# A hybrid attention layer: matmul operands laid out on 256-byte multiples, and one table of distances for eight heads

## The chip, the cores and the metric

One core of a Trainium2 chip runs the whole layer. The metric is device microseconds of one launch. Of the kernel before there are three times and one profiled execution.

## The reference

512 real tokens with 16 learned tokens put ahead (528 positions), width 2048, one layer. The reference, cut to what matters:

```python
h = concatenate([meta, x]); hn = rmsnorm(h, pre_norm_g)
qa, ka, va, ga, qb, kb, vb, gb = split(hn @ w_in)
# mixer A: 8 query heads on 2 key heads, RMSNorm and rotary on q and k
ya = softmax(q @ k.T / sqrt(128)) @ v * silu(ga)
# mixer B: 8 heads, two score maps of width 64 each; slope_h = 2 ** -(h + 1)
s1 = q1 @ k1.T / 8 - slope_h * abs(qpos - kpos)
s2 = q2 @ k2.T / 8 - slope_h * abs(qpos - kpos)
yb = rmsnorm((softmax(s1) - lam * softmax(s2)) @ v, sub_g) * silu(gb)
y = concatenate([ya, yb]) @ w_out
out = (h + rmsnorm(y, post_norm_g))[16:]
```

## The kernel before

All products are made in 32-bit "fp32r" pairs: an operand is split into a high part (a rounded copy, made on ACT) and a low part (what is left, made on DVE), and a product is three matmuls, high·high, low·high and high·low, into one PSUM bank (`three`, L191). So names end in `h` and `l`: `xh`, `xl` are the layer input (16 tiles each, one for each 128 rows of the width, `k` = 0 to 15), `wh`, `wl` a chunk of weights (`wsplit`, L155, from the loaded chunk `st`), `oh`, `ol` the gated heads.

The stages, in order of time:

- **Projection of keys and values** (`dense_T(KEYS)`, L205): weights stand still in TensorE, `xh`/`xl` stream past in two halves of 264 columns (528 positions), into `pd`, in one place into `sc`.
- **Projection of B queries and gates** (`dense_T(REAL)`): the same with the 512 real columns `xh[k][:, NM:]`, which begin 16 columns (64 bytes) into the tile.
- **Projection of A queries** (`queries_A`, L638): `xh`/`xl` stand still, 512 columns of weights stream.
- **Attention** of each head beside these: scores into `sc` (264 columns), turned by `tr` matmuls (128 columns), then `pv` (256 columns). `attention_B` (L440) loads its head's table `dist` of 912 fp16 numbers in each partition (L442) and adds it to the scores on DVE (L460, `p<-sc,dist`).
- **Output projection** (from L804 on): `oh`/`ol` stand still, 512 columns of weights stream into `po`. `dense_out` makes two of the four column blocks plainly; the other two go through a scheme with sums of operands and fewer products (`product`, L899): seven calls, of which `of_y` uses `oh`/`ol`, and `of_t` the sums `uh`, `ul`, `vh`, `vl`.

TensorE's order is fixed by `Lanes`, which weaves the attention of a head into the projection of the next by written estimates of time (`LAG`); it is kept as program order. A list scheduler orders DVE and ACT, with rank for the weight splits. Loads go out in order on SP's queue.

Tiles of a pool are laid end to end in each partition, each rounded up to 32 bytes; pools made with `side="right"` (`xp`, later `op` in its place) are filled back from the top of the memory. `pad` takes a small tile only to shift what follows. So a tile's address follows from the sizes ahead of it: `xh` tiles of 528 numbers are 2112 bytes, 8.25 times 256, and four neighbours begin at four different offsets within 256 bytes.

Of the kernel before, what the change touches and what calls it, by code (L numbers as in the profile page):

```python
# [10 lines left out]
F32 = mybir.dt.float32  # L11
F32R = mybir.dt.float32r
F16 = mybir.dt.float16
AF = mybir.ActivationFunctionType
ALU = mybir.AluOpType
AX = mybir.AxisListType

P = 128
DM = 2048
KT = DM // P  # L20
SEQ = 512
NM = 16
NT = SEQ + NM
# [5 lines left out]
DW = NT + (TT - 1) * P  # L29
# [79 lines left out]
def kernel(ctx: ExitStack, tc: tile.TileContext, xT, xn, xm, w_s, w_t, w_q, w_o,  # L109
                             gpre, gq, gk, lams, gsub, gpost, ident_d, cos_d, sin_d, dist_d, out):  # L110
    nc = tc.nc
# [5 lines left out]
    cst = ctx.enter_context(tc.tile_pool(name="cst", bufs=1))  # L117
# [13 lines left out]
    def ctile(shape, name, dt=F32, src=None, pool=cst):  # L131
        t = pool.tile(shape, dt, name=name, tag=name, bufs=1)
        if src is not None:
            load(t, src)
        return t

    def pad(pool, name):

        pool.tile([P, 8], F32, name=name, tag=name, bufs=1)

    def load(out, in_):

        tc.keep_in_program_order(nc.sync.dma_start(out=out, in_=in_))
# [23 lines left out]
    warm = ctile([P, 1], "warm")  # L167
    nc.scalar.activation(warm, epst, AF.Identity)

    heat = ctile([P, 256], "heat", F32R, pool=ap)  # L170
    nc.vector.memset(heat.bitcast(F32), 0.0)
    hot = pd.tile([P, 512], F32, name="hot", tag="pd")
    for i in range(16):
        mm(hot[:, :256], heat[:, :P], heat, start=True, stop=True)
    gcol = ctile([P, KT], "gcol")
    nc.scalar.dma_start(out=gcol, in_=gpre)
    xh = [xp.tile([P, NT], F32R, name=f"xh{k}", tag=f"xh{k}") for k in range(KT)]
    xl = [xp.tile([P, NT], F32R, name=f"xl{k}", tag=f"xl{k}") for k in range(KT)]
    pad(xp, "xpad")

    def xload(k):
        st = ap.tile([P, NT], F32, name="xs", tag="p", bufs=6)
# [6 lines left out]
    REAL = [(NM, NT)]  # L189
# [15 lines left out]
    def dense_T(segs, pss=None, half=None):  # L205

        pss = pss or [pd.tile([P, 512], F32, name="pd", tag="pd") for _ in segs]
        for k0 in range(0, KT, 8):
            wh, wl = fetch()
            for k in range(k0, k0 + 8):  # L210
                c = slice((k - k0) * P, (k - k0 + 1) * P)
                for (n0, n1), ps in zip(segs, pss):
                    three(ps[:, :n1 - n0], wh[:, c], wl[:, c], k, n0, n1)
                    lanes.poll()
                if half and k == 10:
                    half()
        return pss
# [14 lines left out]
                for (n0, n1), ps in zip(segs, pss):  # L232
                    three(ps[:, :n1 - n0], wh[:, c], wl[:, c], k, n0, n1)

    ones = ctile([P, P], "ones")
    nc.vector.memset(ones, 1.0)
    ones_r = ctile([P, P], "ones_r", F32R)
    nc.vector.memset(ones_r.bitcast(F32), 1.0)
    mhalf = ctile([P, 8], "mhalf")
    nc.vector.memset(mhalf, -0.5)  # L240

# [23 lines left out]
    nc.vector.tensor_tensor(out=rm, in0=ssm[:, 0:1], in1=ssm[:, 1:2], op=ALU.add)  # L265
    rstd(rt, rt, DM)
    rstd(rm, rm, DM, NM)
    pad(cst, "ipad")
    ident = ctile([P, P], "ident", src=ident_d)
    rB = ctile([P, NT], "rB")  # L270
    dg = ap.tile([P, NT], F32, name="dg", tag="tT")
# [14 lines left out]
    sinT = ctile([P, TT, P], "sinT", src=sin_d, pool=ap)  # L286
    gqB = ctile([P, P], "gqB", src=gq, pool=ap)
    gkB = ctile([P, P], "gkB", src=gk, pool=ap)
    pad(cst, "spad")
    sgc = ctile([P, 1], "sgc", src=gsub)  # L290
    nc.vector.tensor_scalar(out=sgc, in0=sgc, scalar1=1.0 - LAMBDA_INIT, scalar2=None,
                            op0=ALU.mult)

    lmt = ctile([P, 4, 64], "lmt", src=lams)
    lpr = ctile([P, 2, 64], "lpr")
    nc.vector.tensor_tensor(out=lpr, in0=lmt[:, 0::2, :], in1=lmt[:, 1::2, :], op=ALU.mult)
    lsm = ctile([P, 2], "lsm")
    nc.vector.tensor_reduce(out=lsm, in_=lpr, op=ALU.add, axis=AX.X)
    nc.scalar.activation(lsm, lsm, AF.Exp)
# [26 lines left out]
        lo(s2[L], kf[U], s2[U])  # L326
        return s1, s2

    def queries_B(pss):
        qf = ap.tile([P, NT], F32, name="qf", tag="tT")  # L330
        qf = qf[:, :SEQ]
        nc.vector.tensor_tensor(out=qf, in0=pss[0], in1=rB[:, NM:], op=ALU.mult)
        q1 = ap.tile([P, SEQ], F32R, name="q1", tag="q1")
        q2 = ap.tile([P, SEQ], F32R, name="q2", tag="q2")
        l1 = ap.tile([P, SEQ], F32R, name="l1", tag="ql", bufs=4)
        l2 = ap.tile([P, SEQ], F32R, name="l2", tag="ql", bufs=4)
        hi(q1[L], qf[L])
        hi(q2[U], qf[U])
        hi(q1[U], qf[L])
        hi(q2[L], qf[U])  # L340
        lo(l1[L], qf[L], q1[L])
        lo(l2[U], qf[U], q2[U])
        lo(l1[U], qf[L], q1[L])
        lo(l2[L], qf[U], q2[U])
        return (q1, l1), (q2, l2)
# [92 lines left out]
        return t.rearrange("p (a b) -> p a b", a=2)  # L438

    def attention_B(h, qs, ks, v, v_task):  # L440
        dist = ap.tile([P, DW], F16, name="dist", tag="dist")
        nc.sync.dma_start(out=dist, in_=dist_d[h])  # L442
        o = ap.tile([P, SEQ], F32, name="oB", tag="f", bufs=4)
        last = None
        for half in range(2):
            pts = []
            for t in (2 * half, 2 * half + 1):
                tq = slice(t * P, (t + 1) * P)
                mx = ap.tile([P, 2], F32, name="mx", tag="mx", bufs=4)
                sm = ap.tile([P, 2], F32, name="sm", tag="sm", bufs=4)  # L450
                p2 = []
                yield from room(2)
                for m, ((q, ql), s) in enumerate(zip(qs, ks)):
                    sc = psc.tile([P, 2, 512], F32, name="sc", tag="sc")
                    for i, (n0, n1) in enumerate(KEYS):
                        mm(sc[:, i, :HALF], q[:, tq], s[:, n0:n1], start=True, stop=False)
                        mm(sc[:, i, :HALF], ql[:, tq], s[:, n0:n1], start=False, stop=True)
                    p = ap.tile([P, NT], F32, name="p", tag="p", bufs=6)
                    w0 = (TT - 1 - t) * P
                    nc.vector.tensor_tensor_reduce(  # L460
                        out=two(p), in0=sc[:, :, :HALF], in1=two(dist[:, w0:w0 + NT]),
                        scale=-0.125, scalar=3.0e38, op0=ALU.add, op1=ALU.min,
                        accum_out=mx[:, m:m + 1])
                    p2.append(p)
                    if m == 0:
                        yield LAG["scB"]
                for m in range(2):
                    nc.scalar.activation(p2[m], p2[m], AF.Exp, scale=-1.0,  # L468
                                         bias=mx[:, m:m + 1], accum_out=sm[:, m:m + 1])
                nc.vector.reciprocal(out=sm, in_=sm)  # L470
                c2 = ap.tile([P, 1], F32, name="c2", tag="c2", bufs=4)
                nc.vector.tensor_tensor(out=c2, in0=sm[:, 1:2], in1=nlam, op=ALU.mult)
                nc.gpsimd.tensor_scalar(out=p2[0], in0=p2[0], scalar1=sm[:, 0:1], scalar2=1.0,  # L473
                                        op0=ALU.mult, op1=ALU.mult)
                nc.vector.scalar_tensor_tensor(out=p2[0], in0=p2[1], scalar=c2, in1=p2[0],
                                               op0=ALU.mult, op1=ALU.add)
                pts.append(p2[0])
                if t % 2 == 0:
                    yield LAG["scB"]
            last = spawn_pv(v_task, p_times_v(pts, v, lambda pv, half=half: nc.scalar.activation(  # L480
                o[:, half * 256:(half + 1) * 256], pv, AF.Copy), None), LAG["pB"])
            if half == 0:
                yield LAG["scB"]
        over[h] = lanes.spawn(finish_B(h, o), LAG["fin"], last)
# [37 lines left out]
    zed = []  # L522
# [52 lines left out]
    def head_norm(raw, n, g, rows=P):  # L575

        ss = ap.tile([P, 4], F32, name="ssh", tag="ssh", bufs=4)
        for i in range(n):
            jk = ap.tile([P, P], F32, name="jk", tag="jk")
            nc.scalar.activation(jk[:rows], raw[:, i, :], AF.Square, accum_out=ss[:rows, i:i + 1])  # L580
        rstd(ss[:rows, :n], ss[:rows, :n], P, rows)
        for i in range(n):
            nc.vector.scalar_tensor_tensor(out=raw[:, i, :], in0=raw[:, i, :],  # L583
                                           scalar=ss[:rows, i:i + 1], in1=g[:rows], op0=ALU.mult,
                                           op1=ALU.mult)
# [15 lines left out]
    def keys_A(pss):  # L601
# [1 line left out]
        for (n0, n1), ps in zip(KEYS, pss):  # L603
            nc.scalar.activation(kf[:, n0:n1], ps[:, :n1 - n0], AF.Copy)
        kn = ap.tile([P, TT, P], F32, name="kn", tag="f", bufs=4)
        km = ap.tile([NM, 1, P], F32, name="km", tag="km")
        kh = ap.tile([P, NT], F32R, name="kh", tag="s1")
        kl = ap.tile([P, NT], F32R, name="kl", tag="s2")

# [128 lines left out]
    sc = psc.tile([P, 2, 512], F32, name="sc", tag="sc")  # L738
    pss = dense_T(KEYS, [sc[:, 0, :], sc[:, 1, :]], spread)
    ks = keys_B(first[0])  # L740
    qs = queries_B(first[1])
    v = values(pss)
    gB = [gate(first[2], "gB0")] + [None] * (NH - 1)
    heads, over = [None] * (2 * NH), [None] * (2 * NH)
# [5 lines left out]
    for h in range(NH):  # L750
        heads[h] = lanes.spawn(attention_B(h, qs, ks, *v), LAG["head"], heads[h - 1])
        if h > 0 and h not in LATE:
            weigh()
            gB[h] = gate(dense_T(REAL), f"gB{h}")
        if h + 1 < NH:
            if h:
                weigh()
            pss = dense_T(KEYS)
            if h:
                finish_head(h - 1)  # L760
            v = values(pss)
            if h:
                weigh()
            ks = keys_B(dense_T(KEYS))
            qs = queries_B(dense_T(REAL))
    kA, vA = [], []
    for i in range(2):
        pss = dense_T(KEYS)
# [1 line left out]
        kA.append(keys_A(pss))  # L770
        vA.append(values(dense_T(KEYS)))
    gA = []
    zed.append(ap.tile([P, DW], F16, name="zed", tag="dist"))
    nc.vector.memset(zed[0], 0.0)
    for grp in range(2):
        qn, q_task = queries_A(grp)
# [14 lines left out]
    op = ctx.enter_context(tc.tile_pool(name="op", bufs=1, side="right", reuse_waits="tile"))  # L791
    oh = [op.tile([P, SEQ], F32R, name=f"oh{j}", tag=f"oh{j}") for j in range(KT)]
    ol = [op.tile([P, SEQ], F32R, name=f"ol{j}", tag=f"ol{j}") for j in range(KT)]
    pad(op, "opad")

    def bring(j):
        st = wp.tile([P, 1024], F32, name="os", tag="st")
# [308 lines left out]
```

## Time and profile before

| | |
|---|---|
| median of 3 runs | 937.16 us (936.48 to 939.98) |
| the profiled execution | 936.8 us, its span 935.0 us |
| TensorE (PE) | 919.7 us busy, 98% of the span, 5498 matmuls |
| weight loads (PEld) | 808.4 us, 86% |
| DVE | 570.8 us, 61% |
| ACT | 489.3 us, 52% |
| POOL | 120.8 us, 13% |
| mean granted TensorE clock | 0.997 |

How to read it: a matmul's busy time is longer than its place in the stream, since matmuls overlap; 512 columns show some 395 ns while the next one starts 230 ns later. What counts is the spacing from start to start, and a row of the chain of waits gives it: its length divided by its count of matmuls. PEld runs beside PE, the weights of the next matmul being loaded while the one before streams.

### The profile page before, as it was taken

Reading aid. Unit: us, or ns where it says so; the run is one execution under the profiler, and the core shown is the slowest. Engines: PE = TensorE matmul, PEld = TensorE weight load, DVE = VectorE, ACT = ScalarE, POOL = GpSimd, SP = SyncE. Lnnn points to the kernel's source line nnn. Section 1 sums busy time; section 2 is a strip of 40 time slices with the busy share of each in tenths; the row PEclk is TensorE's granted clock in tenths of the full one; section 3 lists DMA queues with packets and bytes.
Section 4 is the critical chain, followed back from the end, with each engine's and each line's share of the span. In section 5 each row is a group of like instructions: output and inputs, shape, how many; then the busy total and the mean of one; then the engine's idle time right before and its main releaser. Section 6 shows DMA issues by size and latency. Waiting matters only on the chain.

```text
span 935.0 us, 14280 instructions
## 1 busy us (share of the span) xinstructions
PE 919.7 (98%) x5498; PEld 808.4 (86%) x5498; DVE 570.8 (61%) x1013; ACT 489.3 (52%) x853; POOL 120.8 (13%) x164
## 2 busy tenths in 40 slices
PE   9999999999999999999999999999999999999996
PEld 8989898998989899898999888887888888888884
DVE  6376675747557475765756246447645573654797
ACT  6665564637455474644645244436554662524662
POOL 0001110110101110010111030115211120300110
PEclk9999999999999999999999999999999999999998
DMA  9855534544536365231322223221222163765884
GB/s 336 264 166 146 140 125 117 148 144 134 159 103 180 101 164 150 68 103 68 93 71 87 90 85 96 70 77 57 83 76 69 60 212 94 269 207 160 287 311 181
DMA packets 44260, 129.75 MB, mean 139 GB/s; under 512 B 5120, under 2 KB 9984, under 8 KB 43936
## 3 DMA queue, kind: packets, MB, share of 16 engines
q1 hardware_dynamic: 40784, 117.29, 37.8%
q0 software_dynamic: 3264, 11.54, 6.6%
q8 instruction: 43, 0.70, 0.3%
q14 instruction: 25, 0.20, 0.1%
q10 hardware_dynamic: 144, 0.01, 0.0%
HBM read 120.43 MB, written 25.17 MB: 156 GB/s over the span
## 4 chain that ended last, share of the span: by engine, by line
PE 92%; DVE 3%; issue 1%; ACT 1%; DMA 1%; POOL 0%; DVEq 0%; POOLq 0%; ACTq 0%
PE pd L63 60%; PE po L63 16%; PE sc L63 6%; PE tr L66 5%; PE pv L63 5%; DVE y L995 1%; DMA os<-oscr 1%; DVE wl L159 0%; PE ss L63 0%; DVE l L316 0%; ACT wh L158 0%; DMA gcol<-in_gpre_dram 0%; DVE y L1007 0%; DVE qn L583 0%; POOL ssh L246 0%
## 5 line engine op out<-in xcount | busy, mean ns | idle before, releaser
L63 PE MATMUL pd<-xh,wh 128*128 128x264 f32 (+1 forms) x992 | 332.5, 335 | 0.1
L63 PE MATMUL pd<-xh,wl 128*128 128x264 f32 (+1 forms) x992 | 324.2, 327 | 1.1 <-DVE wl L159 1.0
L63 PE MATMUL pd<-xl,wh 128*128 128x264 f32 (+1 forms) x992 | 324.5, 327 | 0.0
L158 ACT ACTIVATE wh<-st 128x1024 fp32r<-128x1024 f32 (+2 forms) x147 | 152.7, 1040 | 213.5 <-issue 91.5
L159 DVE TENSOR_TENSOR wl<-st,wh 128x1024 fp32r<-128x1024 f32 (+2 forms) x147 | 176.4, 1201 | 120.5 <-ACT wh L158 119.6
L63 PEld LDWEIGHTS pd<-xh,wl 128*128 128x128 f32 x992 | 186.5, 188 | 18.2 <-DVE wl L159 1.5
L63 PEld LDWEIGHTS pd<-xh,wh 128*128 128x128 f32 x992 | 186.9, 188 | 12.8 <-ACT wh L158 0.4
L63 PEld LDWEIGHTS pd<-xl,wh 128*128 128x128 f32 x992 | 187.1, 189 | 11.2 <-DVE xl L185 0.2
L63 PE MATMUL po<-wh,oh 128*128 128x512 f32 x176 | 70.3, 402 | 0.1
L468 ACT ACTIVATE p<-p,mx 128x528 f32<-128x528 f32 x64 | 47.0, 734 | 43.0 <-DVE mx L460 42.7
L63 PE MATMUL po<-wh,ol 128*128 128x512 f32 x176 | 69.0, 395 | 0.2 <-DVE ol L316 0.2
L63 PE MATMUL po<-wl,oh 128*128 128x512 f32 x176 | 69.0, 395 | 0.0
L313 ACT ACTIVATE ph<-tr 128x512 fp32r<-128x512 f32 x64 | 37.7, 590 | 39.1 <-PE tr L66 38.7
L460 DVE CUSTOM_DVE_ANT_0 p<-sc,dist 128x528 f32<-128x528 f32 x64 | 44.8, 700 | 15.3 <-PE sc L63 15.0
L316 DVE TENSOR_TENSOR pl<-tr,ph 128x512 fp32r<-128x512 f32 x64 | 43.4, 687 | 16.6 <-ACT ph L313 16.2
L66 PE MATMUL tr<-ident,p 128*128 128x128 f32 (+1 forms) x320 | 50.6, 272 | 1.7 <-DVE pl L316 1.7
L63 PE MATMUL pd<-wh,xh 128*128 128x512 f32 x128 | 51.9, 406 | 0.0
L63 PE MATMUL pd<-wl,xh 128*128 128x512 f32 x128 | 50.5, 394 | 0.0
L63 PE MATMUL pd<-wh,xl 128*128 128x512 f32 x128 | 50.3, 393 | 0.0
L66 PEld LDWEIGHTS tr<-ident,p 128*128 128x128 f32 (+1 forms) x320 | 37.4, 131 | 13.0 <-DVE pl L316 2.5
L558 POOL TENSOR_SCALAR p<-p,smA 128x528 f32<-128x528 f32 x32 | 26.9, 841 | 144.6 <-DVE smA L557 123.0
L473 POOL TENSOR_SCALAR p<-p,sm 128x528 f32<-128x528 f32 x32 | 23.0, 718 | 168.7 <-DVE sm L470 168.3
(202 smaller groups left out, 1478.2 us busy)
## 6 DMA issues: line engine op xcount, KB each, us to landing
st<-in_w_t_dram SPq DMA_DIRECT2D x82, 512.0 KB, 3.8
st<-in_w_o_dram SPq DMA_DIRECT2D x24, 512.0 KB, 4.0
ws<-in_w_o_dram POOLq DMA_DIRECT2D x16, 512.0 KB, 6.6
st<-in_w_q_dram SPq DMA_DIRECT2D x16, 512.0 KB, 3.5
st<-ws SPq DMA_DIRECT2D x16, 512.0 KB, 4.9
xs<-in_xT_dram SPq DMA_DIRECT2D x16, 264.0 KB, 5.6
xns<-in_xn_dram SPq DMA_DIRECT2D x8, 512.0 KB, 5.2
ws<-in_w_o_dram SPq DMA_DIRECT2D x8, 512.0 KB, 5.3
```

Source lines behind the costliest of these rows:

```text
L63: self._add(self.nc.tensor.matmul(out, lhsT, rhs, start=start, stop=stop), us)
L66: self._add(self.nc.tensor.transpose(out, in_, ident), 0.109)
L158: nc.scalar.activation(wh[:, c], st[:, c], AF.Copy)
L159: nc.vector.tensor_tensor(out=wl[:, c], in0=st[:, c], in1=wh[:, c].bitcast(F32), op=ALU.subtract)
L313: nc.scalar.activation(dst, src, AF.Copy)
L316: nc.vector.tensor_tensor(out=dst, in0=src, in1=h.bitcast(F32), op=ALU.subtract)
L460: nc.vector.tensor_tensor_reduce(out=two(p), in0=sc[:, :, :HALF], in1=two(dist[:, w0:w0 + NT]), scale=-0.125, scalar=3.0e38, op0=ALU.add, ...
L468: nc.scalar.activation(p2[m], p2[m], AF.Exp, scale=-1.0, bias=mx[:, m:m + 1], accum_out=sm[:, m:m + 1])
L473: nc.gpsimd.tensor_scalar(out=p2[0], in0=p2[0], scalar1=sm[:, 0:1], scalar2=1.0, op0=ALU.mult, op1=ALU.mult)
L558: nc.gpsimd.tensor_scalar(out=p, in0=p, scalar1=sm, scalar2=1.0, op0=ALU.mult, op1=ALU.mult)
L995: order(nc.vector.scalar_tensor_tensor(out=v, in0=v, scalar=ry[t], in1=xres[t, g], op0=ALU.mult, op1=ALU.add))
```

## The change

In the built program it moves addresses and leaves TensorE's 5184 rows in the order they had. The offsets below are those of the operands' first byte, modulo 256, worked out from the allocations of both programs; "moving" is the operand that streams, "standing" the one loaded as weights.

| matmuls | moving, standing before | after |
|---|---|---|
| keys, values: 1920 of 264 columns | eight offsets in turn (`xh`/`xl`: 0 and 32, 64 and 96, 128 and 160, 192 and 224), 128 | 192 and 224, 0 |
| B queries, gates: 1152 of 512 | 0, 64, 128 or 192 by `k`, 128 | 0, 0 |
| A queries: 384 of 512 | 128; 0, 64, 128 or 192 by `k` | 0, 0 |
| output with `oh`/`ol`: 528 of 512 | 128, 192 | 0, 0 |
| output with `u`, `v`: 144 of 512 | 128, 128 | 0, 0 |
| last output product, `v`: 48 of 512 | 192, 128 | 0, 0 |
| scores: 448 of 264 | multiples of 32, 128 | multiples of 32, 64 |
| `pv`: 384 of 256 (`ph`/`pl`, `vh`/`vl`) | 0, 128 | 128, 64 |

Room for wider tiles comes from single buffers (`dist`, `jk`, `km`, `zed`), from shared places (`heat` in the place of `pm`, `lmt` in that of `fr`, `ones` and `ones_r` in one) and from the table: head 2's distances (`dist_d[2]`, slope 1/8) are loaded once and serve all eight heads. The B queries are multiplied by `slope(h)` = 2^(h−2) as they leave PSUM, and the scale of L460 is divided by it.

```diff
-    def pad(pool, name):
+    def pad(pool, name, n):
-        pool.tile([P, 8], F32, name=name, tag=name, bufs=1)
+        pool.tile([P, n // 4], F32, name=name, tag=name, bufs=1)
...
-    heat = ctile([P, 256], "heat", F32R, pool=ap)
+    heat = ap.tile([P, 256], F32R, name="heat", tag="pm")
...
-    xh = [xp.tile([P, NT], F32R, name=f"xh{k}", tag=f"xh{k}") for k in range(KT)]
-    xl = [xp.tile([P, NT], F32R, name=f"xl{k}", tag=f"xl{k}") for k in range(KT)]
-    pad(xp, "xpad")
+    xh, xl = [[xp.tile([P, 576], F32R, name=f"x{n}{k}", tag=f"x{n}{k}")[:, :NT]
+               for k in range(KT)] for n in "hl"]
+    pad(xp, "xpad", 32)
...
-    pad(cst, "spad")
+    pad(cst, "spad", 160)
...
+    dist = ap.tile([P, DW], F16, name="dist", tag="dist", bufs=1)
+    pad(ap, "dpad", 32)
+    load(dist, dist_d[2])
+
+    def slope(h):
+        return 2.0 ** (h - 2)
+
-    def queries_B(pss):
+    def queries_B(h, pss):
...
-        nc.vector.tensor_tensor(out=qf, in0=pss[0], in1=rB[:, NM:], op=ALU.mult)
+        nc.vector.scalar_tensor_tensor(out=qf, in0=pss[0], scalar=slope(h), in1=rB[:, NM:],
+                                       op0=ALU.mult, op1=ALU.mult)
...
     def attention_B(h, qs, ks, v, v_task):
-        dist = ap.tile([P, DW], F16, name="dist", tag="dist")
-        nc.sync.dma_start(out=dist, in_=dist_d[h])
...
-                        scale=-0.125, scalar=3.0e38, op0=ALU.add, op1=ALU.min,
+                        scale=-0.125 / slope(h), scalar=3.0e38, op0=ALU.add, op1=ALU.min,
...
-    zed.append(ap.tile([P, DW], F16, name="zed", tag="dist"))
+    zed.append(ap.tile([P, DW], F16, name="zed", tag="dist", bufs=1))
...
-    pad(op, "opad")
+    pad(op, "opad", 224)
```

On SP's queue the constants end with `lmt`, and the weight chunks `st` of the following projections come behind them. Before:

```order
L143 DMA sgc<-in_gsub_dram 128x1
L143 DMA lmt<-in_lams_dram 128x256
L151 DMA st<-in_w_t_dram 128x1024 x3
L442 DMA dist<-in_bias_dram 128x912 x2
L151 DMA st<-in_w_t_dram 128x1024 x5
```

In the changed program:

```order
L143 DMA sgc<-in_gsub_dram 128x1
L143 DMA lmt<-in_lams_dram 128x256
L143 DMA dist<-in_bias_dram 128x912
L151 DMA st<-in_w_t_dram 128x1024 x8
L143 DMA ws_545<-in_w_o_dram 128x1024
```

The one table now stands ahead of three chunks of weights, and the seven other loads of a table are gone from the queue.

On DVE, where the first head's keys are split (`s`) beside the first weights of the next projection (`wl`), the rows before were:

```order
L316 TENSOR_TENSOR s_679<-kf,s_679 64x528
L159 TENSOR_TENSOR wl<-st,wh 128x1024
L316 TENSOR_TENSOR s_680<-kf,s_680 64x528
L316 TENSOR_TENSOR l_689<-qf,q_687 64x512
L159 TENSOR_TENSOR wl<-st,wh 128x1024
```

In the changed program:

```order
L316 TENSOR_TENSOR s_679<-kf,s_679 64x528
L316 TENSOR_TENSOR s_680<-kf,s_680 64x528
L159 TENSOR_TENSOR wl<-st,wh 128x1024
L316 TENSOR_TENSOR l_689<-qf,q_687 64x512
L159 TENSOR_TENSOR wl<-st,wh 128x1024
```

The first `wl` comes one row later, behind both halves of the keys; ACT's rows for the same data (`s` and `wh`) change places in the same way.

More of the change, by code (lines that the diff above doesn't have):

```diff
@@ L233 @@
                     three(ps[:, :n1 - n0], wh[:, c], wl[:, c], k, n0, n1)
-    ones = ctile([P, P], "ones")
+    ones_r = ctile([P, P], "ones_r", F32R)
+    ones = ones_r.bitcast(F32)
     nc.vector.memset(ones, 1.0)
-    ones_r = ctile([P, P], "ones_r", F32R)
-    nc.vector.memset(ones_r.bitcast(F32), 1.0)
     mhalf = ctile([P, 8], "mhalf")
@@ L267 @@
     rstd(rm, rm, DM, NM)
-    pad(cst, "ipad")
+    pad(cst, "ipad", 32)
     ident = ctile([P, P], "ident", src=ident_d)
@@ L292 @@
                             op0=ALU.mult)
-    lmt = ctile([P, 4, 64], "lmt", src=lams)
-    lpr = ctile([P, 2, 64], "lpr")
-    nc.vector.tensor_tensor(out=lpr, in0=lmt[:, 0::2, :], in1=lmt[:, 1::2, :], op=ALU.mult)
+    lmt = ap.tile([P, 4, 64], F32, name="lmt", tag="fr")
+    load(lmt, lams)
+    lpr = lmt[:, 0::2, :]
+    nc.vector.tensor_tensor(out=lpr, in0=lpr, in1=lmt[:, 1::2, :], op=ALU.mult)
     lsm = ctile([P, 2], "lsm")
@@ L578, in head_norm @@
         for i in range(n):
-            jk = ap.tile([P, P], F32, name="jk", tag="jk")
+            jk = ap.tile([P, P], F32, name="jk", tag="jk", bufs=1)
             nc.scalar.activation(jk[:rows], raw[:, i, :], AF.Square, accum_out=ss[:rows, i:i + 1])
@@ L605, in keys_A @@
         kn = ap.tile([P, TT, P], F32, name="kn", tag="f", bufs=4)
-        km = ap.tile([NM, 1, P], F32, name="km", tag="km")
+        km = ap.tile([NM, 1, P], F32, name="km", tag="km", bufs=1)
         kh = ap.tile([P, NT], F32R, name="kh", tag="s1")
@@ L740 @@
     ks = keys_B(first[0])
-    qs = queries_B(first[1])
+    qs = queries_B(0, first[1])
     v = values(pss)
@@ L764 @@
             ks = keys_B(dense_T(KEYS))
-            qs = queries_B(dense_T(REAL))
+            qs = queries_B(h + 1, dense_T(REAL))
     kA, vA = [], []
```

## The prediction

> **What bounds the kernel now.** I read the page's shares first, then the chain of waits, then its pieces inside single stages.
>
> ```profile
> PE 919.7 (98%) x5498; PEld 808.4 (86%) x5498; DVE 570.8 (61%) x1013; ACT 489.3 (52%) x853; POOL 120.8 (13%) x164
> PE 92%; DVE 3%; issue 1%; ACT 1%; DMA 1%; POOL 0%; DVEq 0%; POOLq 0%; ACTq 0%
> ```
>
> PE carries 92% of the chain; no other engine carries more than 3%. So the time is the number of matmuls times their spacing, and a change of addresses can act only through the spacing. Does the spacing depend on addresses? The output projection is the clean place: four stretches of it, one after another, are nothing but 512-column matmuls, and the chain gives length and count (start, length, engine and tile, count).
>
> ```profile
> 799.86 65.33 PE po L63 x280
> 871.96 18.15 PE po L63 x80
> 893.29 10.27 PE po L63 x44
> 904.95 9.76 PE po L63 x43
> ```
>
> The spacings are 233.3, 226.9, 233.4 and 227.0 ns. The first and third stretch read `oh`/`ol` (moving at 128, standing at 192), the second and fourth the sums `u` and `v` (128 and 128). Shape, clock and number of operands are the same, and the spacing goes up and down with the offset. So offsets do cost time. A last stretch has moving 192, standing 128; its first and last row here stand 40 matmuls apart:
>
> ```profile
> 915.47 0.39 PE L63 MATMUL po<-wh,vh 128*128 128x512 f32 x1
> 924.63 0.39 PE L63 MATMUL po<-wh,vl 128*128 128x512 f32 x1
> ```
>
> That is 229.0 ns. I read from it that the difference between the two offsets matters: none gives 226.9, 64 gives 229.0, minus 64 gives 233.3. After the change all 512-column matmuls have difference 0, like the 226.9 stretch, though at 0 and 0 instead of 128 and 128. No matmul at 0 and 0 stands in this trace: that step is an inference.
>
> The remaining 512-column matmuls sit in the projections:
>
> ```profile
> 516.72 56.50 PE pd L63 x243
> 205.54 4.17 PE pd L63 x18
> 436.20 4.20 PE pd L63 x18
> ```
>
> A queries: 232.5 ns. Gates, the first and last of 10 undisturbed 18-matmul pieces in the attention of the B heads: 231.7 and 233.3. I use 232.5 for both. They don't reach 226.9 even where a tile has difference 0, since the offsets change after every 3 or 6 matmuls. Where the `u` stretch begins one sees what a change of offset costs:
>
> ```profile
> 870.87 0.40 PE L63 MATMUL po<-wh,uh 128*128 128x512 f32 x1
> 872.49 0.39 PE L63 MATMUL po<-wh,ul 128*128 128x512 f32 x1
> ```
>
> These are its first and its eighth matmul: seven spacings of 231.4, and only then 226.9. A stream settles.
>
> The Trainium skill, "SBUF — State Buffer", section "SBUF: two separate sides", says that PE has ports of its own and never waits for anyone, and that a port lock between DVE and GpSimd is the only contention on the engine side. By that rule addresses cost nothing and the change gives 937; the four stretches above speak against it, by 6.4 ns a matmul.
>
> **The change part by part.**
>
> *Output projection.* `oh`/`ol` have 528 matmuls. 369 of them stand in the undisturbed stretches (321 in a row, then 48 between the sums): 369 × (233.3 − 226.9) = 2.4 us. The other 159 share PE with the last heads and mostly stay in the first seven after a change: 159 × (233.3 − 231.4) = 0.3 us. The sums in the second and fourth stretch gain nothing. The last product gains 48 × 2.1 = 0.1 us on PE, which I don't count, for the end belongs to DVE:
>
> ```profile
> 914.97 0.60 DVE y L1001
> 922.29 0.60 DVE y L1001
> 930.38 1.32 DVE y L995 x2
> ```
>
> From 914.97 the chain runs on DVE alone. Sum: 2.7 us.
>
> *Gates, B queries, A queries.* 1536 matmuls. In PE's program order, which stays, 570 of them stand later than seventh in a run of their own kind (363 gates and B queries, 207 A queries); the others are in short runs between pieces of attention. 570 × (232.5 − 226.9) + 966 × (232.5 − 231.4) = 3.2 + 1.1 = 4.3 us. Bounds: nothing settles between pieces of attention (all 1536 at 231.4: 1.7 us), or all is settled from the first (226.9: 8.6 us).
>
> *Keys and values.* These 1920 matmuls now all have 192 and 224 against 0. Before, four pairs take turns; `xh2` had that same pair of differences (64 and 96 against 128). One turn from `xh2`, at its four first matmuls and the next `xh6`:
>
> ```profile
> 44.10 0.28 PE L63 MATMUL sc<-xh,wh 128*128 128x264 f32 x1
> 44.83 0.28 PE L63 MATMUL sc<-xh,wh 128*128 128x264 f32 x1
> 45.55 0.29 PE L63 MATMUL sc<-xh,wh 128*128 128x264 f32 x1
> 46.27 0.28 PE L63 MATMUL sc<-xh,wh 128*128 128x264 f32 x1
> 47.00 0.28 PE L63 MATMUL sc<-xh,wh 128*128 128x264 f32 x1
> ```
>
> Six matmuls each: 0.73, 0.72, 0.72, 0.73 us. The pair that remains is one of the dearer: 121.7 against the turn's mean of 2.90 / 24 = 120.8; if it keeps its price, 1920 × 0.9 = 1.7 us are lost. In the output projection difference 64 was not dear once settled, so I take half of this, 0.9 us lost, between 1.5 us gained (all as cheap as 0.72 / 6 = 120.0) and 3.3 us lost (0.73 may be 0.735: 122.5).
>
> *Scores and `pv`.* The score operands still take turns over multiples of 32; `pv` goes from difference 128 to 64. Neither has a long stretch to read. I take 0, ± 0.5 us (800 matmuls, ± 0.6 ns, the spread of the pairs above).
>
> *The table.* Seven loads go. Nobody waited for one: the score operation's idle time is PE's.
>
> ```profile
> L460 DVE CUSTOM_DVE_ANT_0 p<-sc,dist 128x528 f32<-128x528 f32 x64 | 44.8, 700 | 15.3 <-PE sc L63 15.0
> dist<-in_bias_dram SPq DMA_DIRECT2D x8, 228.0 KB, 2.8
> 45.63 1.11 SPq L442 DMA_DIRECT2D dist<-in_bias_dram  x2
> ```
>
> Gain 0. One load moves ahead of three weight chunks on SP: 0.55 us of issue later for them. The multiplication by the slope makes 8 tensor-tensor operations into three-operand ones:
>
> ```profile
> L332 DVE TENSOR_TENSOR qf<-pd,rB 128x512 f32<-128x512 f32 x8 | 5.5, 690 | 30.8 <-PE pd L63 30.8
> L508 DVE SCALAR_TENSOR_TENSOR gB<-oB,sgc,gB 128x512 f32<-128x512 f32 x8 | 5.9, 739 | 0.0
> ```
>
> 8 × 49 ns = 0.4 us on an engine that is 61% busy and sits idle for PE ahead of just this line; the scores of the head come later. 0, at most 0.4. The clearing of `zed` now waits for head 7's last score operation, on the same engine, and A's first score comes after.
>
> *The moved row.* The first `wl` of the next projection now stands behind one more `s`, and PE waits there:
>
> ```profile
> 52.12 0.70 DVE L316 TENSOR_TENSOR s<-kf,s 64x528 fp32r<-64x528 f32 x1
> 52.85 1.22 DVE L159 TENSOR_TENSOR wl<-st,wh 128x1024 fp32r<-128x1024 f32 x1
> 58.93 0.77 DVE L307 TENSOR_TENSOR vf<-sc,rB 128x264 f32<-128x264 f32 x2
> 54.13 0.40 PE L63 MATMUL pd<-xh,wl 128*128 128x264 f32 x1 [0.99 <-DVE wl L159]
> 59.42 0.89 PE L66 MATMUL tr<-ident,vf 128*128 128x128 f32 x4 [1.25 <-DVE vf L307]
> ```
>
> PE starts 0.70 us later at 54.13. But it waits again for `vf` at 59.42, 1.25 us long, and DVE's rows up to `vf` are the same in sum; so the second wait shrinks to 0.55 and the cost is 0. That wait is the cover; were it gone, 0.7 us.
>
> *Sharing bytes.* `oh0` now lies over `xh3` and `xh4` instead of `xh0` and `xh1`, so its first writer must wait for later matmuls.
>
> ```profile
> 741.09 1.39 PE pd L63 x6
> 741.62 0.63 ACT L313 ACTIVATE oh<-os 128x512 fp32r<-128x512 f32 x1
> ```
>
> The last gate ends at 742.48; after `xh4` it has 11 tiles with 3 matmuls, at least 7.7 us at 232.5, so `xh4` was free by 734.8, before that write. Cost 0.
>
> *The sum.* −2.7 − 4.3 + 0.9 = −6.1 us: span 928.9, and the profiled execution's 936.8 becomes 930.7. The median of the runs stands 0.4 us above it, so **931 us**. The ends of the unknown terms together: gains of 2.7 + 8.6 + 1.5 + 0.5 = 13.3, to 924; at the other ends 2.7 + 1.7 − 3.3 − 0.5 − 0.4 = 0.2 is left, 937.
>
> **The rivals.**
>
> *Nothing to measure (935 to 937).* The 6.4 ns belong to something else in the two kinds of stretch, or the 264-column matmuls lose what the others gain: 3.3 + 0.9 us lost against 4.4 gained, if nothing settles. For it: only 369 matmuls have a like-for-like row, and they alone bring 2.4 us. Against it: the stretches alternate twice, between calls of the same function. The skill's rule of the separate ports, above, comes to this rival.
>
> *Much faster (below 924).* Offset 0 removes the rest of the excess as well. From 264 columns at 120.8 to 512 at 226.9 a column costs 0.428 ns, and 512 of these with nothing fixed beside them are 219 ns. The 2208 matmuls on the path have a mean of 232.2 now (1536 at 232.5, 528 at 233.3, 144 at 226.9, with a little rounding): 2208 × 13.2 = 29 us, to 908; half of it 922. For it: each operand then starts on a 256 boundary, which no row has. Against it: 226.9, 229.0 and 233.3 order themselves by difference alone, and nothing settled lies lower. The Trainium skill, "TensorE: Matmul & The Clock Gate", section "Back-to-back issue gap", gives N / 2.4 + 2.5 ns for an isolated warm matmul, 216 ns for 512 columns at any address; by that figure the most to be had would be an estimated 36 us, to 901, and no stretch of this trace agrees with it.
>
> *Slower (above 942).* At 0 and 0 moving and standing stream begin in the same place and hinder each other more than at 128 and 128, all the time since all share it. It decides from a rise of (4.7 − 0.9) / 2208 = 1.7 ns, to a mean of 233.9; at 238 it is 2208 × 5.8 + 0.9 us = 13.7 us, 951. For it: a standing state, once bad, would no longer be broken up by changing offsets. Against it: 128 and 128 is the best row in the trace.
>
> **How the numbers follow.** Forecast 0.60, nothing to measure 0.21, much faster 0.11, slower 0.08. 0.5% is 4.7 us, about what a measurement of this kernel can tell from no change, so below 932.5 counts as faster. The forecast's own range, 925 to 935.5, lies on that side with about 0.50 of its 0.60. Faster is 0.50 + 0.11 = 0.61, same 0.10 + 0.21 = 0.31, slower 0.08. The range 923.5 to 937 leaves out the slower case and most of the much faster one.
>
> **What would show it.** Right: `po` pieces of the chain near 226.9 in all long stretches; the 243-matmul piece of A queries near 227 to 229; 18-matmul pieces of gates near 4.12 us; keys at 120.5 to 121.7; the wait for `wl` longer and that for `vf` shorter by 0.7. Wrong: `po` at any other spacing than 227, which falsifies the rule of the difference; keys above 122; or a new wait of PE for DVE.

## The result, and the profile after

The changed kernel takes 928.47 us (median of 5 runs, 927.5 to 928.56), against 937.16 us for the kernel before (936.48 to 939.98): a ratio of 0.9898, interval 0.9887 to 0.991, so 8.7 us less. The profiled executions stand at 928.5 and 936.8 us, spans 926.7 and 935.0.

The page's shares and the chain's shares, which answer to the first two rows of the prediction:

```profile
PE 912.6 (98%) x5498; PEld 807.3 (87%) x5498; DVE 571.0 (62%) x1012; ACT 491.8 (53%) x853; POOL 116.6 (13%) x164
PE 90%; DVE 4%; ACT 2%; issue 2%; DMA 1%; POOL 1%; SPq 0%; DVEq 0%; ACTq 0%; POOLq 0%
```

The same 5498 matmuls, and PE is still the bound; it is busy for 7.1 us less. The chain inside the output projection (start, length, engine and tile, count), stretch by stretch as before:

```profile
790.87 71.86 PE po L63 x317
862.95 18.13 PE po L63 x80
884.71 10.43 PE po L63 x46
895.59 9.52 PE po L63 x42
```

These are 226.7, 226.6, 226.7 and 226.7 ns a matmul. The first and third, which read `oh`/`ol`, were at 233.3 and 233.4; now no seam between the four can be seen. A queries, and the first and last undisturbed pieces of gates in the B heads:

```profile
515.03 55.31 PE pd L63 x243
205.18 4.09 PE pd L63 x18
434.39 4.10 PE pd L63 x18
```

227.6, 227.2 and 227.8 ns, where 232.5, 231.7 and 233.3 stood. Keys, pieces of 24 matmuls:

```profile
113.43 2.88 PE pd L63 x24
172.33 2.92 PE pd L63 x24
```

120.0 and 121.7 ns; pieces of the kernel before were at 2.90 and 2.92 us. PE's waits, all of 0.4 us and more, before:

```profile
PE tr L66 <- DVE pl L316: 1.7, 2, 1.5
PE tr L66 <- DVE vf L307: 1.2, 1, 1.2
PE hot L63 <- DVE heat L171: 1.2, 1, 1.2
PE pd L63 <- DVE wl L159: 1.0, 1, 1.0
PE tr L66 <- DVE gA L563: 0.5, 1, 0.5
```

and after (us in total, times, longest):

```profile
PE hot L63 <- DVE heat L171: 1.2, 1, 1.2
PE pd L63 <- DVE wl L159: 1.0, 1, 1.0
PE tr L66 <- DVE vf L307: 0.6, 1, 0.6
PE pd L63 <- DVE xl L185: 0.4, 1, 0.4
PE pd L63 <- ACT wh L158: 0.4, 1, 0.4
PE sc L63 <- DVE qlA L316: 0.4, 1, 0.4
```

To see where the 8.3 us between the two profiled executions went, each matmul of the one trace was laid beside the same matmul of the other, and the time from its start to the next start was summed by kind. A wait is booked to the matmul ahead of it; "undisturbed" is the mean of the spacings without such a wait.

| matmuls | sum before, us | after, us | difference | undisturbed spacing, ns |
|---|---|---|---|---|
| gates and B queries, 1152 | 274.38 | 268.84 | −5.5 | 232.4 → 228.9 |
| A queries, 384 | 90.62 | 89.56 | −1.1 | 231.8 → 228.9 |
| output with `oh`/`ol`, 528 | 125.50 | 122.64 | −2.9 | settled: 233.3 → 226.8 |
| output with `u`, `v`, 192 | 43.47 | 43.29 | −0.2 | last product: 229.2 → 226.7 |
| keys, values, 1920 | 240.84 | 241.71 | +0.9 | 121.3 → 121.3 |
| scores | 55.09 | 56.32 | +1.2 | 121.6 → 121.1 |
| `pv` | 49.56 | 49.05 | −0.5 | 118.8 → 117.8 (384 of 416) |

With some 0.3 us less in the warm-up (`hot`) and the `ss` sums, that is −8.4, rounding included.

### The profile page after: what moved, and what is told of

It reads as the page before. It is cut to its first block, busy times and chain, and to the rows that moved or that the text cites. A ratio compares the mean times of both kernels' runs of the same rounds, so it can differ in the third digit from the quotient of the medians.

```text
span 926.7 us, 14251 instructions
## 1 busy us (share of the span) xinstructions
PE 912.6 (98%) x5498; PEld 807.3 (87%) x5498; DVE 571.0 (62%) x1012; ACT 491.8 (53%) x853; POOL 116.6 (13%) x164
## 4 chain that ended last, share of the span: by engine, by line
PE 90%; DVE 4%; ACT 2%; issue 2%; DMA 1%; POOL 1%; SPq 0%; DVEq 0%; ACTq 0%; POOLq 0%
PE pd L63 58%; PE po L63 16%; PE sc L63 6%; PE tr L66 5%; PE pv L63 5%; DVE y L1003 1%; DVE wl L159 1%; DMA xs<-in_xT_dram 1%; DMA os<-oscr 1%; PE ss L63 0%; DVE l L316 0%; ACT wh L158 0%; POOL ssh L245 0%; ACT jk L588 0%; DVE y L1015 0%
## 5 line engine op out<-in xcount | busy, mean ns | idle before, releaser
L159 DVE TENSOR_TENSOR wl<-st,wh 128x1024 fp32r<-128x1024 f32 (+2 forms) x147 | 176.5, 1201 | 118.9 <-ACT wh L158 117.8
L566 POOL TENSOR_SCALAR p<-p,smA 128x528 f32<-128x528 f32 x32 | 23.7, 741 | 145.5 <-DVE smA L565 119.0
```

Of the source, the lines that this page charges most:

```text
L159: nc.vector.tensor_tensor(out=wl[:, c], in0=st[:, c], in1=wh[:, c].bitcast(F32), op=ALU.subtract)
L566: nc.gpsimd.tensor_scalar(out=p, in0=p, scalar1=sm, scalar2=1.0, op0=ALU.mult, op1=ALU.mult)
```

## The experiments

The theory: the spacing of a 512-column matmul depends on the difference between the offsets of its moving and its standing operand within 256 bytes, and on nothing else that was changed. The rivals: the gain comes from the one table of distances and the work it saves; or from operands that begin on a 256 boundary; or from the gates' tiles alone.

**Only the table.** The kernel before with one table for all heads. The operands of all 512-column matmuls and of keys and values keep their addresses. Those of the scores and `pv` move, since `dist` is now allocated earlier; `pv` comes to difference 64, as in the changed kernel.

```diff
+    dist = ap.tile([P, DW], F16, name="dist", tag="dist")
+    load(dist, dist_d[2])
...
-        nc.vector.tensor_tensor(out=qf, in0=pss[0], in1=rB[:, NM:], op=ALU.mult)
+        nc.vector.scalar_tensor_tensor(out=qf, in0=pss[0], scalar=slope(h), in1=rB[:, NM:],
+                                       op0=ALU.mult, op1=ALU.mult)
...
-                        scale=-0.125, scalar=3.0e38, op0=ALU.add, op1=ALU.min,
+                        scale=-0.125 / slope(h), scalar=3.0e38, op0=ALU.add, op1=ALU.min,
```

> The kernel before with one table of distances alone; every address of a matmul operand stays as it was. If the difference of the offsets is the cause: no change, 936.5 to 937.5 us, output stretches at 233.3 and 226.9 ns as before. If the seven loads less and the changed order on DVE make the gain: 928 to 930 us.

Measured: 936.95 us, ratio 0.9996 (0.9987 to 1.0005). The chain in the first output stretch:

```profile
799.88 72.80 PE po L63 x312
```

233.3 ns, as before. The table is worth nothing that can be measured in time; what it gives is room.

**Everything moved by 128.** The changed kernel, with three paddings altered so that every operand of a 512-column projection or output matmul begins 128 bytes past a 256 boundary, all differences kept at 0 (keys and values keep 192 and 224).

```diff
-    pad(xp, "xpad", 32)
+    pad(xp, "xpad", 160)
-    pad(cst, "spad", 160)
+    pad(cst, "spad", 32)
-    pad(op, "opad", 224)
+    pad(op, "opad", 352)
```

> The changed kernel with everything moved by 128 bytes (weights, x tiles, heads, sums), so that differences stay and no operand of a 512-column matmul begins on a 256 boundary. If only the difference counts: as the changed kernel, 928 to 929 us, 226.7 ns in all output stretches. If beginning on a boundary counts: slower, up to 937 us, with output stretches above 227 ns.

Measured: 928.23 us, ratio 0.9899 (0.9885 to 0.9913). The first output stretch:

```profile
790.96 70.95 PE po L63 x313
```

226.7 ns at 128 and 128, as at 0 and 0. None of these operands is on a boundary, and the gain is all there. So the boundary is not what counts.

**Weights moved by 64, and by 128.** The changed kernel with only the padding ahead of the weights' and sums' buffers altered. The difference becomes +64 (+128) for the output with `oh`/`ol` and the A queries, −64 (−128) for the gates, and stays 0 for the sums `u` and `v` ahead of the last product, which move along with the weights. (The last product comes to −64 and −128.)

```diff
-    pad(cst, "spad", 160)
+    pad(cst, "spad", 224)
```

> The changed kernel with weights and sums moved by 64 bytes and x tiles and heads left: difference +64 for the output and A queries, -64 for gates and B queries, 0 in the products of the sums. Difference theory: 229.0 ns in the output stretch with heads, 226.7 with sums u and v, gates near 233 ns; 528 matmuls of the output 0.8 us, gates and B queries 4 us, A queries 0.5 us, keys and values 1 us dearer: 934 to 936 us. Boundary theory: stretches with sums lose as well. Table theory: 928.5 us.

Measured: 934.37 us, ratio 0.9961 (0.9948 to 0.9974). The output stretch, then the sums:

```profile
796.86 70.50 PE po L63 x308
868.28 10.88 PE po L63 x48
```

228.9 and 226.7 ns. The gates' settled spacing, at −64, was 233.0. Both figures for 64, which the prediction had read from one stretch each, came back on matmuls that had been elsewhere; two neighbouring stretches differ by what was moved.

With 288 in place of 224, for 128:

> The same with 128 bytes: difference 128 for all 512-column matmuls but the sums'. Difference theory: the output stretch with heads settles somewhere in 231 to 234 ns (difference 128 was seen only in short runs, mean 232.4), sums stay at 226.7 though at 128 and 128; 934 to 937 us. If the period of the effect were 128 bytes and not 256: 226.7 ns and 928.5 us. Table theory: 928.5 us.

Measured: 935.62 us, ratio 0.9978 (0.997 to 0.9987). The output stretch:

```profile
797.00 72.03 PE po L63 x310
```

232.4 ns. So 128 is not as good as 0, and the pattern does not repeat within 256 bytes at 128.

**Only the output's padding.** The kernel before, with the 32 bytes ahead of `oh`/`ol` made 96. `oh` and `ol` come to 128, like the weights, and the last product's weights do too.

```diff
-    pad(op, "opad")
+    op.tile([P, 24], F32, name="opad", tag="opad", bufs=1)
```

> The kernel before with the pad ahead of the heads' tiles alone changed, so that oh and ol stand at 128 like the weights that stream past them. Difference theory: the output stretches with heads fall from 233.3 to 226.7 ns and nothing else moves; gain 369 x 6.6 ns + 159 x 2 ns = 2.8 us, 934.3 us. Boundary theory: 937 us, since nothing begins on a 256 boundary.

Measured: 934.62 us, ratio 0.997 (0.9959 to 0.9982), 2.8 us below the kernel before on its chip (937.4). The first stretch:

```profile
797.00 71.42 PE po L63 x315
```

226.7 ns. This one line of the kernel, alone, gives what the whole change gives in this stage: matched one by one, the matmuls with `oh`/`ol` take 2.9 us less and the last product 0.2 less.

**The tiles of the input narrow again.** The changed kernel with `xh`/`xl` of 528 numbers, laid end to end as before, so that gates and A queries go through the four differences by `k`.

```diff
-    xh, xl = [[xp.tile([P, 576], F32R, name=f"x{n}{k}", tag=f"x{n}{k}")[:, :NT]
+    xh, xl = [[xp.tile([P, NT], F32R, name=f"x{n}{k}", tag=f"x{n}{k}")[:, :NT]
```

> The changed kernel with x tiles of 528 numbers again, so that their offsets take turns; the rest stays. Difference theory: gates and B queries back to 232.4 ns (4.0 us), A queries to 231.8 (1.1 us), keys and values unchanged in the mean (121.3 ns), output stretches at 226.7: 933.5 us. Together with the kernel that moves the heads' tiles alone this should account for the whole 8.7 us within 1 us. Table theory: 928.5 us.

Measured: 932.55 us, ratio 0.9949 (0.9937 to 0.9961). A queries, and the output:

```profile
517.77 56.52 PE pd L63 x243
796.79 69.36 PE po L63 x306
```

232.6 and 226.7 ns. Gates and A queries are back at their old spacing; the output keeps its gain. Wide tiles are so worth 4.1 us against the changed kernel (3.8 if both are first set against the kernel before on their own chips), and with the 2.8 us of the run above some 6.9 of the 8.7 us are accounted for by one edit each. I had expected all 8.7 within 1 us, so this missed; it came out 1 us lower than I expected. Its gates sum to 272.42 us at the old spacing, where the kernel before has 274.38: the 2 us of waits for `pl` and `gA` are gone here too, so these waits hang on neither the wide tiles nor the gates' spacing, and they are about what the two edits leave unaccounted.

**Keys in 272 and 256 columns.** If the difference of offsets were what a 264-column matmul pays for as well, the second half should start at difference 0, 272 numbers or 1088 bytes into the tile. The first half then has 272 columns. All else is as in the changed kernel.

```diff
+    PARTS = [(0, 272), (272, NT)]
...
-        pss = dense_T(KEYS)
+        pss = dense_T(PARTS)
```

> The changed kernel with keys and values projected in 272 and 256 columns instead of 264 and 264: the second part then begins at 0 like the weights (difference 0), the first stays at 192. Difference theory, with the prices that a 264-column matmul had before at these differences (121.0 at 192, 120.2 at 0): 272 columns 124.4 ns, 256 columns 116.8 ns, 960 x 1.35 ns = 1.3 us gained, 927.2 us. If differences don't matter to matmuls this short: 928.5 us.

Measured: 930.87 us, ratio 0.9931 (0.9918 to 0.9944): 2.4 us slower than the changed kernel, where I had looked for a gain. Two pieces of keys:

```profile
64.59 2.95 PE pd L63 x24
113.06 2.96 PE pd L63 x24
```

122.9 and 123.3 ns on average, against 120.0 to 121.7. Matched one by one, the 256-column half takes 119.5 ns at difference 0, the 272-column half 125.9 at 192: together 245.4 against 242.6 for two halves of 264. The 8 columns more cost the first half 4.9 ns; the second half, 8 columns shorter and at difference 0, gains only 2.1, to 119.5 where I had expected 116.8. The rule of the 512-column stream gave no gain on matmuls of half its length.

**Weights moved by 32, and by 96.** One execution each, since the question is the spacing and not the time. 192 in place of 160 for 32 bytes:

```diff
-    pad(cst, "spad", 160)
+    pad(cst, "spad", 192)
```

> The changed kernel with weights and sums moved by 32 bytes: difference +32 for the output and A queries, -32 for gates and B queries. Difference theory: a settled spacing between 226.7 and 233.3 ns for each sign, never seen so far; if spacing grows with the distance of the offsets, near 228 and 230 ns. Sums stay at 226.7. If only multiples of 64 count: 226.7 ns for both signs and 928.5 us.

Measured: 935.87 us beside 937.40 for the kernel before. The output stretch, then the sums:

```profile
796.90 72.80 PE po L63 x312
870.39 10.65 PE po L63 x47
```

233.3 and 226.6 ns. If the cost grew with the distance it would have been near 228; 32 bytes cost more than 64.

256 in place of 160, for 96 bytes:

> The changed kernel with weights and sums moved by 96 bytes: difference +96 for the output and A queries, -96 (160) for gates and B queries; the last two differences of the eight that 32-byte steps allow. Difference theory: settled spacings above 226.7 ns for both signs, by the 64 and 32 byte runs between 229 and 233.4; sums at 226.7; 934 to 937 us. If a difference other than 0 is better: below 226.7 ns in one of the stretches. Table theory: 928.5 us.

Measured: 940.81 us beside 937.15, slower than the kernel before and above the 934 to 937 that I expected. The output, and two pieces of keys:

```profile
801.91 72.56 PE po L63 x311
66.13 2.99 PE pd L63 x24
174.66 2.99 PE pd L63 x24
```

233.3 ns again, and keys at 124.6. Here the 264-column matmuls are the dear part: 245.41 us in sum against 241.52 with 32 bytes. Their differences are 96 and 128, which also occur in the two runs with 64 and 128 bytes, at 122.0 and 121.2 ns; here they take 124.0 and 122.8. So for them the difference alone does not set the price. What else does, no run tells apart.

## Why the prediction was right, point by point

The median forecast was 931, and 928.5 was measured; the sum was −6.1 us and the profiled executions differ by −8.3.

*Output projection, −2.7.* Measured −2.9 with `oh`/`ol`, and 2.8 us for that padding alone. The inference on which it stood, that 0 and 0 would be as good as 128 and 128, is shown by the run that moved everything by 128: the settled output stretches of the two differ by less than 0.1 ns. The last product went from 229.2 to 226.7 ns, and the end still belongs to DVE; PE's last matmul starts at 917.19, 9.5 us ahead of the span's end both before and after, so this 0.1 us counted after all.

*Gates, B queries, A queries, −4.3.* This is the mis-sized step. Without waits the 1536 matmuls gained 1152 × 3.4 + 384 × 2.9 ns = 5.1 us; with the waits booked to them 6.6. The rule "seven matmuls at 231.4, then 226.9" was read from a stream that had come from another difference. Where all differences are 0, position by position in the trace of after: the first three matmuls of a run stand at 231.0 to 231.3 ns, the fourth to ninth at 227.7 to 230.0, the tenth and later at 226.7 (some 1000 of them). A short piece between two parts of attention settles from the fourth on, and the 966 matmuls that I took for unsettled did not stay at 231.4. The 243 A queries at 227.6 and the gates' pieces at 4.09 and 4.10 us (I named 4.12) show it.

*Keys and values, +0.9.* The sum rose by 0.87, but not for my reason. Undisturbed, they went from 121.34 to 121.27 ns: the pair that remains costs 121.0 and 121.6, and is not one of the dearer. Nor is the rise the moved row's: start to start, what is lost before `wh` and `wl` (0.72) and what is regained before `vf` (0.69) both stand among these matmuls and cancel. What remains is the wait for `xl` at 8 us, 0.42 idle and 0.77 with the spacings beside it, and 0.26 ahead of a turn of `vf` at 482 us. The wait for `xl` stands in some of the programs here and not in others (it is 0.42 with the narrow tiles too, and absent with everything moved by 128). Half of 1.7 us was a guess that waits filled, so the agreement of this term is luck.

*The moved row, 0.* The sum is as written, the place of the wait is not: the one for `wl` stayed at 1.05 us, and the new part stands ahead of it, for `wh` on ACT. On DVE and PE after the change:

```profile
52.68 1.44 DVE L316 TENSOR_TENSOR s<-kf,s 64x528 fp32r<-64x528 f32 x2
54.15 1.23 DVE L159 TENSOR_TENSOR wl<-st,wh 128x1024 fp32r<-128x1024 f32 x1
53.87 0.39 PE L63 MATMUL pd<-xh,wh 128*128 128x264 f32 x1 [0.40 <-ACT wh L158]
55.43 0.39 PE L63 MATMUL pd<-xh,wl 128*128 128x264 f32 x1 [1.05 <-DVE wl L159]
59.97 0.89 PE L66 MATMUL tr<-ident,vf 128*128 128x128 f32 x4 [0.56 <-DVE vf L307]
```

Both `s` stand ahead of `wl`, PE waits 0.40 + 1.05 where it waited 0.99, and the wait for `vf` falls from 1.25 to 0.56: 0.46 lost, 0.69 regained. The cover held.

*Scores and `pv`, 0.* `pv` gained 0.5 us, the end of its range: 118.8 to 117.8 ns as its difference went from 128 to 64 (117.3 with only the table, where it is 64 too). The scores lost 1.2, most of it (0.8) at one wait, named below, and none through undisturbed spacing, which fell by 0.5 ns.

*What was not in the sum.* In A's first heads the kernel before waits for `pl` (1.50 us) and `gA` (0.55):

```profile
642.87 0.66 PE L66 MATMUL tr<-ident,qn 128*128 128x128 f32 x4 [0.55 <-DVE gA L563]
645.73 0.66 PE L66 MATMUL tr<-ident,p 128*128 128x128 f32 x4 [1.50 <-DVE pl L316]
```

After the change `pl` stands ahead of the steps that prepare the next queries on DVE, and PE waits for those instead:

```profile
643.22 0.39 PE L63 MATMUL sc<-kh,qlA 128*128 128x264 f32 x1 [0.40 <-DVE qlA L316]
```

The prediction had named a new wait of PE for DVE as a sign of being wrong; this one and that for `xl` are such waits, outweighed by those that left. Term by term, what the sum lacks: gates and A queries fell by 6.6 where 4.3 stood, 0.8 of the difference by spacing and 1.5 by waits; `pv` gives 0.5, the output 0.4 (0.2 of it the last product), warm-up and `ss` 0.3; the scores take 1.2 back. That is 2.3, against 2.2 between −6.1 and −8.3. The run with only the table still has the old wait for `pl`, the run with narrow tiles has the new one; which of the other edits reorders DVE here was not taken apart. The prediction looked at DVE's order at 52 us and did not look at it here.

*The table, 0.* Shown by its own run, 936.95. *Sharing bytes, 0.* No wait of `oh`'s writer for PE stands in the trace.

*The rivals.* Nothing to measure fell with the ratio's interval, and with it the rule of the Trainium skill, "SBUF — State Buffer", section "SBUF: two separate sides", as far as it would have PE never wait: with all else alike, 64 bytes of padding cost 5.9 us (934.37 against 928.47). Whether this is one engine waiting for another, of which that section speaks, or PE's two operands meeting each other, no run shows. Much faster did not come: every settled stretch of every run, wherever it lay, has 226.7 ns as its floor, and the 216 ns of the Trainium skill, "TensorE: Matmul & The Clock Gate", section "Back-to-back issue gap", given there for an isolated matmul, stand in none. (The mean that this rival starts from, 232.2 ns, comes to 232.3 from its own figures; its 29 us stay.) Slower has its mechanism refuted: 0 and 0 does not hinder itself more than 128 and 128.

## What to carry to other kernels

Where the chain runs on matmuls, compare the settled spacing of stretches with the same shape before asking for fewer matmuls: two neighbouring stretches at 233.3 and 226.9 ns were the whole clue. Then work out the first bytes of the moving and the standing operand; for 512 columns of 4 bytes give them the same offset within 256 bytes, by one padding tile where a buffer is alone (2.8 us for one line here), and by rounding the tile up where many tiles follow each other (about 4 us). Don't carry the rule to shorter matmuls without measuring: 256 columns at difference 0 with 272 at 192 lost 2.4 us here.

## What the runs showed of the hardware that was not expected

Settled spacing of a 512-column matmul in ns (tenth of a run and later), by the difference moving minus standing, in bytes modulo 256, over all runs of this study:

| difference | output, `oh`/`ol` | A queries | gates | last product |
|---|---|---|---|---|
| 0 | 226.7 | 226.8 | 226.7 | 226.7 |
| 32 | 233.3 | 233.4 | | |
| 64 | 229.0 | 229.0 | | 228.9 |
| 96 | 233.3 | 233.3 | | |
| 128 | 232.3 | 232.2 | 232.6 | 233.3 |
| 160 | | | 233.7 | 234.3 |
| 192 | 233.3 | | 233.0 | 233.3 |
| 224 | | | 233.4 | 233.3 |

(The row of 160 comes from the run with 96 bytes, in which the sums, at difference 0, stood at 226.9 too and not at 226.7.) It is no slope: 0 is alone at the bottom, 64 is in between, and all others lie within 2.1 ns of each other. At 0, 32, 64 and 96 the same difference gives the same spacing in every place, with weights streaming; from 128 on places differ by up to 1.1 ns. Moving both operands by 128 changes nothing, and the sums `u` and `v`, which moved together with the weights to 32, 64, 96 and 128, stood at 226.7, 226.7, 226.9 and 226.7 ns. Nor do whole steps of 256 count: the gates of the changed kernel, with tiles 2304 bytes apart, go through differences of 0, 256, 512 and 768 within 1024 bytes and settle at 226.6 to 226.8 ns at each. What in the chip makes it so, whether the reading of the two operands or the loading of weights beside the stream, was not tried and stays open; the weight loads themselves show 187 to 188 ns in all these stretches, the slow ones too.
